# Low parts of w_o and of the second block's routing moved from GpSimd to VectorE

## Chip, cores and metric

One Trainium2 chip, one core. The metric is the device time of one execution in microseconds; lower is better. Times of several executions are given with their median. A profile is one further execution, recorded by the hardware profiler.

## The reference, cut to what matters

A stack of two blocks on 256 tokens of width 1024, in float32. The first is one hybrid layer, the second has two layers, of which the second layer's feed-forward part is a mixture of 8 experts.

```python
# first block
x = x + concat([mla_out, rw_out]) @ w_o                 # w_o: 1024 x 1024
x = x + hier_moe(rms_norm(x, g_ffn), ...)               # 32 small experts
# second block, i = 0, 1
mix = concat([y_pool, y_conv]) @ w_out[i]
x = layer_norm(DEEPNORM_ALPHA * x + mix, ...)
f = swiglu(x, ...) if i == 0 else moe_swiglu(x, ...)
x = layer_norm(DEEPNORM_ALPHA * x + f, ...)
x = x + sigmoid(x @ ple_gate_w[i]) * (p[i] @ ple_w[i])

def moe_swiglu(h, w_router, w1, w3, w2):                # 8 experts of width 3584
    logits = t @ w_router
    top_vals, top_idx = top_k(logits, 2)
    gates = sum(one_hot(top_idx, 8) * softmax(top_vals)[..., None], axis=1)
    for e in range(8):
        out = out + gates[:, e:e+1] * swiglu(t, w1[e], w3[e], w2[e])
```

DEEPNORM_ALPHA is the square root of 2 (4 to the power 0.25).

## The kernel before

Tokens lie on the 128 partitions, in NT = 2 tiles; the residual x is one SBUF tile of 128 x 2 x 1024. Matrix products are made from split operands: `K.split` (L92 to L101) makes a high part `whi` with a Copy on ScalarE (L99), rounded to float32r, and a low part `wlo` = raw - whi with a tensor_tensor on VectorE, or on the engine that it is handed (L100). `mm3` (L113 to L115) then adds three products, high by high, high by low and low by high. With `parts=4` a split is made in four instructions of each engine instead of one. Weights come through `K.load` (L85) into a few `raw` buffers on the SP queue unless another queue is named; a buffer is loaded anew once its readers are done. There are six or fewer raw and two to four split buffers in a stage; in the experts of the second block eight and four.

The program is written with tiles, and a planner that goes by estimated durations puts the instructions of each engine in order; within an engine they then run in that order. `K.behind(list)` (L103) orders the instructions of its block behind the given ones, as far as these are on the same engine.

The stages that the change touches:

- **The end of the first mixer**, `mixer1`. The recurrent half's rows y are normalised (L762 to L771, the last a multiplication with the reciprocal root on VectorE), transposed on TensorE (L776), scaled on ScalarE (L778) and combined on VectorE (L780, L781), and split. Then `w_o(nh, h)` loads and splits quarters of w_o, of 512 rows by 512 columns (tile 128 x 2048). The first two, nh = 0, are made `ahead`, with their low parts on GpSimd. The attention half's rows (L587, L592, L594) are transposed (L794) and split (L796, L797). `finish` multiplies (L113 to L115) and adds into x (L812). The load of w_o(1, 1) is issued from GpSimd's queue. After it come the first block's routing (L899 to L988), its gather (L1046) and its 32 experts (L1074, L1105), whose weights are read unsplit.
- **The routing of the second block's experts**, `moe`. Logits come from TensorE (L1534). `xs` is x split into high and low parts, in rows (L1539, and L1540, L1551, L1552 for the low parts). The logits are transposed (L1545), and `top2` (L833 to L837) finds the two largest of each row, giving A; three small products (L1554 to L1557) count the places, `slot` (L1558, L1559) and `cnt` (L1561). `gather(e)` makes one-hot rows `hot` (L1571) and, in `fill`, 32 matmuls (L1581) that pick an expert's rows, with the high part copied out by ScalarE (L1583) and the low part by VectorE (L1584).
- **The first weight tiles of the experts**, `take`. A tile is 128 x 1792. `jobs` is the list of pairs of tiles in the order of use; `ahead(n)` loads and splits a pair one job before its use. The first two pairs are made before the loop: three of the four tiles with low parts on GpSimd, in pieces of 128 x 448, all but the first behind the high part of xs and the hot rows. Then come the weights of the two experts of each token (`top2_weights`, L846 to L855) and the scaling of x by ALPHA on GpSimd (L1805). The first addition of an expert's result to x (L1661) is at the end of expert 0.

In the experts, `up` multiplies (L1606 if at most 64 tokens are routed to the expert, else L1609), L1837 copies the results out, L1638 turns them, L1822 to L1829 make the hidden rows and L1630 multiplies with w2.

Of the kernel before, what the change touches and what calls it, by code (L numbers as in the profile page):

```python
# [9 lines left out]
F32R = mybir.dt.float32r  # L10
I32 = mybir.dt.int32
U32 = mybir.dt.uint32
AF = mybir.ActivationFunctionType
# [3 lines left out]
ADD, SUB, MUL = ALU.add, ALU.subtract, ALU.mult  # L17
MAX, MIN, EQ = ALU.max, ALU.min, ALU.is_equal

P = 128  # L20
# [3 lines left out]
TOK = 256  # L24
# [151 lines left out]
def mixer1(K, a, x, late, beside):  # L176


    nc, tc = K.nc, K.tc
    with ExitStack() as ctx:  # L180
# [63 lines left out]
        g = nc.gpsimd  # L244
# [32 lines left out]
        for lev in range(6):  # L277
            b = 1 << lev
# [37 lines left out]
        for t in range(NT):  # L316
            ps = K.ps()
            for c in range(KC):
                w = halves[c // 4]
# [9 lines left out]
        for t in range(NT):  # L329
            ps = K.ps()  # L330
# [5 lines left out]
        for c in range(4):  # L336
            ps = K.ps()
            nc.tensor.matmul(ps[:, :TOK], a2[64:128, c * P:(c + 1) * P], lora[64:128, 0, :], start=True, stop=True)
            nc.scalar.activation(ag[:, c, :], ps[:, :TOK], AF.Sigmoid, bias=cols["a0"][:, c:c + 1])
        for c in range(0, 4, 2):  # L340
            ps = K.ps()
# [9 lines left out]
        for c in range(4):  # L351
            ps = K.ps()
# [71 lines left out]
        for t in range(NT):  # L424
            for i, (o, n) in enumerate(((0, 256), (256, 128))):
                z = lat[:, t, o:o + n]
                nc.vector.tensor_scalar(z, z, lss[:, i, t:t + 1], None, op0=MUL)
        for m in range(4):
            ps = K.ps()
# [62 lines left out]
        for i, gcol in enumerate((cols["g_cq"][:, 0:1], cols["g_cq"][:, 1:2], cols["g_ckv"][:, 0:1])):  # L492
            ps = K.ps(ps_mla)
# [109 lines left out]
        for t in range(NT):  # L603
            HG.append(K.t(poolB, [P, 8, P]))
            GR.append([K.t(poolB, [P, 8, 64]) for _ in range(2)])
            for par in range(2):
                for j in range(2):
                    ps = K.ps()
# [164 lines left out]
        for m in range(4):  # L773
# [11 lines left out]
        w_o = lambda nh, h, engine=None: K.split(  # L785
            K.load(a["w_o"][0, h * 512:(h + 1) * 512, nh * 512:(nh + 1) * 512], 4, 512, queue=nc.gpsimd if nh and h else None),
            engine=engine)
        ahead = [w_o(0, h, nc.gpsimd) for h in range(2)]
        attend(1, qT1)
        beside(tmp)  # L790
        for m in range(4):
# [338 lines left out]
class Block2:  # L1130
# [378 lines left out]
    def moe(self, cap=P):  # L1509
# [27 lines left out]
        xs = self.pair((P, NT, D))  # L1537
        for t in range(NT):
            rows = [nc.scalar.activation(xs[0][:, t, :], x[:, t, :], AF.Copy).ins]  # L1539
        nc.gpsimd.tensor_tensor(xs[1][:, 0, :], x[:, 0, :], xs[0][:, 0, :], op=SUB)  # L1540
        lT = self.W([P, 512], "sg", bufs=1)[:E, :TOK]
        nc.vector.tensor_copy(lT, ps[:E, :TOK])
        lg = K.ps()
# [3 lines left out]
        nc.vector.tensor_copy(lt, lg[:, :NT * E].rearrange("p (t e) -> p t e", t=2))  # L1547
        A, comb, slot = self.T([P, NT, E], F32R), self.T([P, NT, E]), self.T([P, NT, E])
        tops = [top2(K, self.tmp, lt[:, t, :], iota, A[:, t, :]) for t in range(NT)]
        with K.behind([tops[1][2]]):  # L1550
            nc.vector.tensor_tensor(xs[1][:, 1, :512], x[:, 1, :512], xs[0][:, 1, :512], op=SUB)  # L1551
        nc.gpsimd.tensor_tensor(xs[1][:, 1, 512:], x[:, 1, 512:], xs[0][:, 1, 512:], op=SUB)  # L1552
        ps = K.ps()
        nc.tensor.matmul(ps[:, :2 * E], K.upper_r, A.rearrange("p t e -> p (t e)"), start=True, stop=False)  # L1554
        nc.tensor.matmul(ps[:, E:2 * E], K.ones_r, A[:, 0, :], start=False, stop=True)
# [11 lines left out]
        def gather(e):  # L1567

            h = self.W([P, NT, P], "hot", F32R)
            for t in range(NT):  # L1570
                self.hot = [nc.vector.tensor_scalar(h[:, t, :], slots, slot[:, t, e:e + 1], None, op0=EQ).ins]  # L1571
            g = self.W([P, KC * TOK], f"xg{e % 2}", F32R, 1).rearrange("p (k i s) -> p k i s", i=2, k=KC)

            def fill():
                for k in range(0, KC, 2):
                    ps = K.ps()
                    for i in range(2):
                        for q in range(2):
                            o = (2 * i + q) * P
                            for t in range(NT):  # L1580
                                nc.tensor.matmul(ps[:, o:o + P], xs[i][:, t, (k + q) * P:(k + q + 1) * P], h[:, t, :],  # L1581
                                                 start=(t == 0), stop=(t == NT - 1))
                    nc.scalar.activation(g[:, k:k + 2, 0], ps[:, :TOK].rearrange("p (q s) -> p q s", s=P), AF.Copy)  # L1583
                    nc.vector.tensor_copy(g[:, k:k + 2, 1], ps[:, TOK:].rearrange("p (q s) -> p q s", s=P))  # L1584
                return g, h
            return fill

# [180 lines left out]
        nc.vector.tensor_copy(cnti, cnt)  # L1768


        def take(n, e, s, k, **how):
            w = K.load(down_of(e, s, k) if n == "down" else up_of(n, e, s, k), 1, MS)
            if n == "down":
                return k, [z[:, 0] for z in (K.split(w) if k < 4 else (w,))]
            b = lambda z: z.rearrange("p k (b q) -> p (k b) q", b=4)
            hl = K.split(b(w), **how)
            return k, [z.rearrange("p b q -> p (b q)") for z in hl]

        jobs = []
        for i in range(E * NS + 1):  # L1780
# [8 lines left out]
        def ahead(n):  # L1789

            if n < len(jobs) and n not in taken:
                name, e, s, ks = jobs[n]
                taken[n] = [take(name, e, s, k) for k in ks]

        for n in range(2):
            name, e, s, ks = jobs[n]
            taken[n] = []
            for i, k in enumerate(ks):
                with K.behind(rows + self.hot if n or i else None):
                    taken[n].append(take(name, e, s, k, parts=PARTS, engine=None if (n, i) == (1, 0) else nc.gpsimd))  # L1800
        gs = {0: fill()}
        for t in range(NT):
            with K.behind(K.last):
                top2_weights(K, self.tmp, *tops[t][:2], iota, comb[:, t, :])
                nc.gpsimd.tensor_scalar(x[:, t, :], x[:, t, :], ALPHA, None, op0=MUL)  # L1805
        fewer = self.T([P, E])
        nc.vector.tensor_scalar(fewer, cnt, HALF + 0.5, None, op0=ALU.is_lt)
        most, mosti = self.T([P, 1]), self.T([P, 1], I32)
# [30 lines left out]

        for n, (name, e, s, ks) in enumerate(jobs):  # L1840
            ahead(n + 1)
            i = NS * e + s
            tiles = taken.pop(n)
            q = min(ks)
            if name == "down":
                if s == 0 and q == 0:
                    accs[e] = [K.ps() for _ in range(2)]
                if i == E * NS - 1 and q == 4:
                    for c in range(0, 2 * R, 4):
                        pts = [K.ps() for _ in range(2)]  # L1850
                        arms(e, lambda few: [turn(few, rows, pt, c) for rows, pt in zip(ups[i], pts)])
                        turned(i, c, pts)
                arms(e, lambda few: [down(few, s, hT[i], accs[e], *t) for t in tiles])
                if s == NS - 1 and q == 0:
                    hotT = transposed(e, gs[e][1])
                if s == NS - 1 and q == 2:
                    if e == E - 1:
                        finish_last(e, accs.pop(e), hotT)
                    else:
                        ends = finish(e, accs.pop(e), hotT)  # L1860
                        next(ends)
                continue
            first = name == "exp_w1_2"
            if (e, s, q, first) == (E - 2, 1, 0, True):
                past()
            if q == 0:
                banks = [K.ps() for _ in range(4)]
            g = gs[e][0]
            before = first and i > 0
            if before:  # L1870
                pts = [K.ps() for _ in range(2)]
                turns = lambda few: [turn(few, rows, pt, 2 * q) for rows, pt in zip(ups[i - 1], pts)]
                if s == 0:

                    arms(e - 1, turns)

            def f(few):
                if before and s:
                    turns(few)
                for t in tiles:  # L1880
                    up(few, e, g, banks, *t)
            arms(e, f)
            if before:
                turned(i - 1, 2 * q, pts)
            if q == 6:
                z = evict(banks, "gs" if first else "us")
                ups.setdefault(i, []).append(z)
                if not first and s == NS - 1 and e + 1 < E:
                    gs[e + 1] = gather(e + 1)()
            if first and q in (2, 6):  # L1890
                next(ends, None)
# [75 lines left out]
```

## Time and profile before

| what | value |
|---|---|
| median of 3 runs | 1967.86 us |
| lowest and highest run | 1962.56, 1967.99 us |
| the profiled execution | 1963.39 us |
| its span in the profile | 1961.8 us |
| TensorE matmul busy | 1768.9 us (90%) |
| VectorE busy | 1315.1 us (67%) |
| ScalarE busy | 1092.3 us (56%) |
| GpSimd busy | 169.4 us (9%) |
| DMA | 546.62 MB, mean 279 GB/s |

Busy times are shares of one span over stages with different limits: an engine that is busy for a ninth of the span can be the only one at work in a short stretch. In the views PE is TensorE, PEld its weight loads, DVE is VectorE, ACT ScalarE, POOL GpSimd, and SPq the DMA queue of SyncE. L12 is line 12 of the kernel; for what a helper issues it is the helper's line, so L99 and L100 are the high and low parts of all splits.

### The profile page before, as it was taken

The page shows a single profiled execution, that of the slowest core. Times are in us where ns is not written, and L with a number is a line of the kernel's source. Part 1 is how long each engine was busy: PE and PEld are TensorE (multiplying, and loading weights), DVE is VectorE, ACT ScalarE, POOL GpSimd, SP SyncE. Part 2 cuts the span into 40 slices and gives each one's busy share as a digit, 9 for nine tenths or more (in the row PEclk, how much of TensorE's full clock was granted, in tenths as well). Part 3 has the DMA queues.
Part 4 walks back from the last instruction along what each step waited for, and adds up shares of the span by engine and source line. Part 5 has one row for each costly group of instructions (what it writes and reads, how often), then busy time and mean ns, then how long its engine had stood idle before and what let it go on. Part 6 is the DMA issues. An engine that isn't in the chain of part 4 may idle for free. (4 is left out here: it accounts for less than half of the span.)

```text
span 1961.8 us, 28227 instructions
## 1 busy us (share of the span) xinstructions
PE 1768.9 (90%) x10999; PEld 1421.1 (72%) x10999; DVE 1315.1 (67%) x1619; ACT 1092.3 (56%) x1446; POOL 169.4 (9%) x250
## 2 busy tenths in 40 slices
PE   7988688778899999889899999998999998888997
PEld 6878474333778999788787687787877778767766
DVE  5675641111886445895886586788978679888877
ACT  6444341001474444555675576677868568777773
POOL 3051210000510000052300000000000000000002
PEclk8989689989999999999899999999999999999999
DMA  7000579999844555334699788999999899999993
GB/s 225 30 1 1 183 311 380 422 421 406 297 142 156 192 193 194 134 103 161 244 323 341 266 330 334 366 337 414 408 375 378 308 356 346 402 374 378 416 392 108
DMA packets 131007, 546.62 MB, mean 279 GB/s; under 512 B 13569, under 2 KB 46476, under 8 KB 118541
## 3 DMA queue, kind: packets, MB, share of 16 engines
q1 hardware_dynamic: 126604, 539.21, 72.3%
q10 hardware_dynamic: 3952, 3.84, 0.6%
q8 instruction: 130, 2.13, 0.4%
q0 software_dynamic: 272, 1.05, 0.2%
q14 instruction: 49, 0.39, 0.1%
HBM read 543.01 MB, written 1.05 MB: 277 GB/s over the span
## 5 line engine op out<-in xcount | busy, mean ns | idle before, releaser
L100 DVE TENSOR_TENSOR wlo<-raw,whi 128x1792 fp32r<-128x1792 f32 (+2 forms) x476 | 811.6, 1736 | 212.5 <-ACT whi L99 207.5
L99 ACT ACTIVATE whi<-raw 128x1792 fp32r<-128x1792 f32 (+3 forms) x500 | 692.5, 1425 | 136.5 <-PE ps L1609 49.3
L1606 PE MATMUL ps<-whi,xg 128*128 128x256 f32 (+1 forms) x960 | 279.1, 319 | 14.0 <-ACT sg L1828 13.4
L1606 PE MATMUL ps<-wlo,xg 128*128 128x256 f32 (+1 forms) x960 | 276.5, 317 | 6.9 <-DVE wlo L100 6.5
L1609 PE MATMUL ps<-whi,xg 128*128 128x512 f32 (+1 forms) x768 | 227.6, 376 | 2.4 <-ACT sg L1828 2.4
L1606 PEld LDWEIGHTS ps<-whi,xg 128*128 128x128 f32 x960 | 196.9, 205 | 27.8 <-ACT sg L1828 15.3
L1606 PEld LDWEIGHTS ps<-wlo,xg 128*128 128x128 f32 x960 | 196.4, 205 | 21.9 <-DVE wlo L100 14.7
L1609 PEld LDWEIGHTS ps<-whi,xg 128*128 128x128 f32 x768 | 143.0, 192 | 30.7 <-ACT sg L1828 2.6
L114 PE MATMUL ps<-xTl,whi 128*128 128x256 f32 x576 | 162.6, 283 | 1.4 <-DVE xTl L100 1.4
L115 PE MATMUL ps<-xTh,wlo 128*128 128x256 f32 x544 | 154.1, 284 | 2.7 <-DVE wlo L100 2.6
L113 PE MATMUL ps<-xTh,whi 128*128 128x256 f32 x544 | 152.4, 283 | 0.4 <-ACT xTh L99 0.4
L1609 PE MATMUL ps<-wlo,xg 128*128 128x512 f32 (+1 forms) x384 | 142.5, 371 | 0.0
L1630 PE MATMUL ps<-raw,hd 128*64 128x512 f32 (+3 forms) x512 | 137.6, 542 | 2.1 <-DVE hd L1829 2.1
L100 POOL TENSOR_TENSOR wlo<-raw,whi 128x448 fp32r<-128x448 f32 (+3 forms) x24 | 39.9, 1688 | 1063.8 <-PE ps L1656 968.9
L114 PEld LDWEIGHTS ps<-xTl,whi 128*128 128x128 f32 x576 | 109.0, 189 | 3.5 <-DVE xTl L100 2.3
L1630 PEld LDWEIGHTS ps<-raw,hd 128*64 128x64 f32 (+1 forms) x512 | 62.8, 158 | 64.6 <-issue 54.5
L115 PEld LDWEIGHTS ps<-xTh,wlo 128*128 128x128 f32 x544 | 103.1, 190 | 5.0 <-DVE wlo L100 4.8
L113 PEld LDWEIGHTS ps<-xTh,whi 128*128 128x128 f32 x544 | 102.7, 190 | 1.7 <-ACT xTh L99 0.9
L1105 PE MATMUL ps<-dn,hT 128*32 128x512 f32 x256 | 69.8, 660 | 19.8 <-DMA dn<-in_w_down_dram 19.7
L1609 PEld LDWEIGHTS ps<-wlo,xg 128*128 128x128 f32 x384 | 73.7, 192 | 13.9 <-issue 0.5
L1822 ACT ACTIVATE odd<-ps,t 128x256 f32<-128x256 f32 (+1 forms) x128 | 53.7, 442 | 36.2 <-PE ps L1638 35.8
L1606 PE MATMUL ps<-wlo,hT 128*128 128x256 f32 (+1 forms) x240 | 67.8, 313 | 5.4 <-issue 2.9
(532 smaller groups left out, 2999.9 us busy)
## 6 DMA issues: line engine op xcount, KB each, us to landing
raw<-in_exp_w_dram SPq DMA_DIRECT2D x384, 896.0 KB
raw<-in_dense_w_dram SPq DMA_DIRECT2D x33, 1024.0 KB
gu<-in_w_up_dram SPq DMA_DIRECT2D x32, 1024.0 KB
dn<-in_w_down_dram SPq DMA_DIRECT2D x32, 1024.0 KB
gu<-in_w_gate_dram SPq DMA_DIRECT2D x29, 1024.0 KB
raw<-in_w_in_dram SPq DMA_DIRECT2D x19, 1024.0 KB
raw<-in_w_out_dram SPq DMA_DIRECT2D x8, 1024.0 KB
raw<-in_ple_gate_w_dram SPq DMA_DIRECT2D x8, 1024.0 KB
```

The lines of the kernel that those rows point to most:

```text
L99: self.last = [nc.scalar.activation(hi[o], src[o], AF.Copy).ins, (engine or nc.vector).tensor_tensor(lo[o], src[o], hi[o], op=SUB).ins]
L100: (engine or nc.vector).tensor_tensor(lo[o], src[o], hi[o], op=SUB).ins]
L113: mm(out, a[0], b[0], start=first, stop=False)
L114: mm(out, a[0], b[1], start=False, stop=False)
L115: return mm(out, a[1], b[0], start=False, stop=last).ins
L1105: nc.tensor.matmul(ps[32 * e:32 * e + 32, :], hT[:, k, 32 * e:32 * e + 32], wd[e][:, k, hs], start=(k == 0), stop=(k == 1))
L1606: mm(to[:, o:o + m], few_rows, w[q][:, i.start + o:i.start + o + m], start=first and o == 0 and q == 0, stop=last and o + m == n and q == 1)
L1609: mm(to, rows[:, a_], w[b_][:, i], start=first and q == 0, stop=last and q == 2)
L1630: mm(to[o], hd[1][:, R + r, ::2 if few else 1], w[0][:, i], start=False, stop=False)
L1822: nc.scalar.activation(odd, z[:, :, :, 1], AF.Copy, scale=fewer[:, i // NS:i // NS + 1])
```

## The change

Low parts of the first two quarters of w_o are made by VectorE. In the second block's routing both low parts of xs are made by VectorE, each right behind its high part in the program's text, with no order demanded. The first four weight tiles are loaded, and split in whole tiles: high parts on ScalarE behind the high part of xs, low parts on VectorE behind the hot rows. For expert 0, the gather's low part is copied out by ScalarE. `top2_weights` stands behind the last of the four low parts. The scaling of x goes to VectorE, in the jobs 4 and 5 of the loop, each behind the newest split.

```diff
-        ahead = [w_o(0, h, nc.gpsimd) for h in range(2)]
+        ahead = [w_o(0, h) for h in range(2)]
...
         for t in range(NT):
             rows = [nc.scalar.activation(xs[0][:, t, :], x[:, t, :], AF.Copy).ins]
-        nc.gpsimd.tensor_tensor(xs[1][:, 0, :], x[:, 0, :], xs[0][:, 0, :], op=SUB)
+            nc.vector.tensor_tensor(xs[1][:, t, :], x[:, t, :], xs[0][:, t, :], op=SUB)
...
         tops = [top2(K, self.tmp, lt[:, t, :], iota, A[:, t, :]) for t in range(NT)]
-        with K.behind([tops[1][2]]):
-            nc.vector.tensor_tensor(xs[1][:, 1, :512], x[:, 1, :512], xs[0][:, 1, :512], op=SUB)
-        nc.gpsimd.tensor_tensor(xs[1][:, 1, 512:], x[:, 1, 512:], xs[0][:, 1, 512:], op=SUB)
...
-                    nc.vector.tensor_copy(g[:, k:k + 2, 1], ps[:, TOK:].rearrange("p (q s) -> p q s", s=P))
+                    low = (g[:, k:k + 2, 1], ps[:, TOK:].rearrange("p (q s) -> p q s", s=P))
+                    if e:
+                        nc.vector.tensor_copy(*low)
+                    else:
+                        nc.scalar.activation(*low, AF.Copy)
...
-        def take(n, e, s, k, **how):
+        def take(n, e, s, k):
...
-            b = lambda z: z.rearrange("p k (b q) -> p (k b) q", b=4)
-            hl = K.split(b(w), **how)
-            return k, [z.rearrange("p b q -> p (b q)") for z in hl]
+            return k, [z[:, 0] for z in K.split(w)]
...
+        raws = [K.load(up_of(name, e, s, k), 1, MS)[:, 0] for name, e, s, ks in jobs[:2] for k in ks]
+        highs, lows = [K.t(K.spl, [P, 1, MS], F32R, tag="whi")[:, 0] for _ in raws], [K.t(K.spl, [P, 1, MS], F32R, tag="wlo")[:, 0] for _ in raws]
+        with K.behind(rows):
+            for w, z in zip(raws, highs):
+                nc.scalar.activation(z, w, AF.Copy)
+        with K.behind(self.hot):
+            for w, z, lo in zip(raws, highs, lows):
+                K.last = [nc.vector.tensor_tensor(lo, w, z, op=SUB).ins]
         for n in range(2):
-            name, e, s, ks = jobs[n]
-            taken[n] = []
-            for i, k in enumerate(ks):
-                with K.behind(rows + self.hot if n or i else None):
-                    taken[n].append(take(name, e, s, k, parts=PARTS, engine=None if (n, i) == (1, 0) else nc.gpsimd))
+            taken[n] = [(k, [highs[2 * n + i], lows[2 * n + i]]) for i, k in enumerate(jobs[n][3])]
         gs = {0: fill()}
         for t in range(NT):
             with K.behind(K.last):
                 top2_weights(K, self.tmp, *tops[t][:2], iota, comb[:, t, :])
-                nc.gpsimd.tensor_scalar(x[:, t, :], x[:, t, :], ALPHA, None, op0=MUL)
...
         for n, (name, e, s, ks) in enumerate(jobs):
             ahead(n + 1)
+            if n in (4, 5):
+                with K.behind(K.last):
+                    nc.vector.tensor_scalar(x[:, n - 4, :], x[:, n - 4, :], ALPHA, None, op0=MUL)
```

## Rows read from the trace of the kernel before

**Rows 1.** The page's first line.

```profile
span 1961.8 us, 28227 instructions
```

**Rows 2.** Busy us by stretch: PE, PEld, DVE, ACT, POOL; granted clock; DMA.

```profile
230.00:235.00 5.00, 0.99 (x4) 0.59 (x4) 5.00 (x1) 0.00 (x0) 4.97 (x2) 0.50 0.89 322
...
290.00:295.00 5.00, 5.00 (x49) 1.79 (x51) 1.68 (x9) 1.85 (x3) 0.00 (x0) 1.00 0.00 0
...
400.00:450.00 50.00, 39.48 (x200) 14.23 (x193) 6.76 (x17) 4.28 (x8) 0.00 (x0) 0.90 1.01 421
...
930.00:940.00 10.00, 0.92 (x6) 0.82 (x6) 9.56 (x16) 3.75 (x7) 9.04 (x8) 0.73 0.29 93
...
950.00:1000.00 50.00, 50.00 (x248) 42.11 (x247) 39.54 (x25) 38.38 (x34) 3.33 (x2) 0.98 0.86 320
```

**Rows 3.** TensorE's waits (total, times, longest) and its timeline before L1554.

```profile
PE ps L776 <- DVE TX L771: 10.3, 2, 5.6
...
PE ps L1606 <- ACT sg L1828: 13.4, 7, 2.4
...
939.26 0.39 PE L1554 MATMUL ps<-t,t 128*128 128x16 f32 x1 [9.08 <-DVE t L837]
```

**Rows 4.** VectorE's timeline, second routing: start, busy us, instruction, idle before.

```profile
939.13 0.68 DVE L1551 TENSOR_TENSOR xTl<-t,xTh 128x512 fp32r<-128x512 f32 x1
...
954.19 2.02 DVE L100 TENSOR_TENSOR wlo<-raw,whi 128x1792 fp32r<-128x1792 f32 x1 [2.23 <-ACT whi L99]
```

**Rows 5.** VectorE's timeline, end of the first mixer.

```profile
226.24 9.44 DVE L771 TENSOR_TENSOR TX<-TX,rstd 128x512 f32<-128x512 f32 x2 [1.20 <-ACT rstd L155]
236.85 0.43 DVE L780 TENSOR_TENSOR fin<-fin,t 128x256 f32<-128x256 f32 x1 [1.17 <-ACT fin L778]
...
254.12 2.29 DVE L100 TENSOR_TENSOR wlo<-raw,whi 128x2048 fp32r<-128x2048 f32 x1 [9.78 <-ACT whi L99]
```

**Rows 6.** GpSimd's timeline, end of the first mixer.

```profile
224.77 4.50 POOL L100 TENSOR_TENSOR wlo<-raw,whi 128x2048 fp32r<-128x2048 f32 x1 [42.80 <-ACT whi L99]
...
230.62 4.50 POOL L100 TENSOR_TENSOR wlo<-raw,whi 128x2048 fp32r<-128x2048 f32 x1
```

**Rows 7.** VectorE's timeline in the first routing.

```profile
276.43 0.29 DVE L942 CAST gf<-gi 128x8 f32<-128x8 uint32 x2
...
277.53 0.31 DVE L833 MAX8 m<-em 128x8 f32<-128x32 f32 x2
...
278.10 1.87 DVE L835 CAST f<-i 128x8 f32<-128x8 uint32 x2
...
280.22 0.41 DVE L837 SCALAR_TENSOR_TENSOR t<-iotf,f,o 128x32 fp32r<-128x32 f32 x2
```

**Rows 8.** ScalarE's timeline at both places.

```profile
226.22 1.89 ACT L99 ACTIVATE whi<-raw 128x2048 fp32r<-128x2048 f32 x1
...
928.94 2.00 ACT L1539 ACTIVATE xTh<-t 128x1024 fp32r<-128x1024 f32 x2 [0.89 <-PE ps L1534]
...
952.46 1.70 ACT L99 ACTIVATE whi<-raw 128x1792 fp32r<-128x1792 f32 x1 [3.81 <-PE ps L1609]
```

**Rows 9.** TensorE's timeline: first w_o matmul, first of the gather, first of expert 0.

```profile
244.40 0.80 PE L113 MATMUL ps<-whi,t 128*128 128x512 f32 x1 [2.20 <-DVE t L797]
...
941.17 1.09 PE L1581 MATMUL ps<-hot,xTh 128*128 128x128 f32 x4 [0.89 <-ACT whi L99]
...
948.03 0.73 PE L1609 MATMUL ps<-whi,xg 128*128 128x512 f32 x1
```

**Rows 10.** Busy us by stretch of 1 us, columns as in rows 2.

```profile
934.00:935.00 1.00, 0.00 (x0) 0.00 (x0) 1.00 (x2) 0.00 (x0) 1.00 (x2) 0.82 0.94 394
...
951.00:952.00 1.00, 1.00 (x5) 0.76 (x5) 0.96 (x2) 0.00 (x0) 1.00 (x1) 0.65 0.69 288
```

**Rows 11.** The chain that ended last: start, us, what.

```profile
1764.62 0.84 PE ps L1581 x8
```

## Prediction

> **What bounds the kernel now.** I read the page first, for the span, then the busy time by stretch, then what TensorE waited for, and only then the timelines of the engines at the two places that the diff touches. The span is 1961.8 us and the profiled execution took 1963.39, so 1.6 us lie around it [rows 1]. Read by stretch, the kernel is a chain of stages with different limits. In the experts of the second block TensorE is busy all the time (50.00 of 50 us from 950), and in the experts of the first block the DMA engines are full (1.01, 421 GB/s). Two short stretches have neither: in 230 to 235 and in 930 to 940 TensorE works about 1 us, while VectorE and GpSimd are both full [rows 2]. The waits say whom TensorE stood for: 10.3 us for VectorE's L771 and 9.1 us, from 930.2 to 939.3, for its L837 [rows 3]. These are two narrow places in a serial chain, so a microsecond saved there is a microsecond of the end, if what follows moves along.
>
> Why VectorE is slow there is to be seen by laying two timelines side by side. L771 is two instructions on 128x512; the same kind and size takes 0.68 us undisturbed [rows 4], here the two take 9.44 [rows 5]. GpSimd's two low parts of 4.50 us run from 224.77 and from 230.62, to 235.12, and L771 ends at 235.68 [rows 6]. So a GpSimd tensor_tensor holds VectorE's instructions up until it ends. The same shows in the first routing: two CASTs of 128x8 take 0.29 us, and beside GpSimd's L955 1.87 [rows 7].
>
> **First edit, the low parts of w_o.** Removed: two GpSimd instructions, and with them the hold-up, 9.44 less 2 x 0.68 = 8.1 us. Added: the same two low parts on VectorE, 2.29 us each by the row of the same shape, together 4.6 us [rows 5]. Where they come in VectorE's order decides. The first high part is there before the square root is; the second only at 226.22 + 1.89 = 228.1 [rows 8]. VectorE has two holes nearby: 1.20 us before L771 and 1.17 us after it, in which it waits for ScalarE [rows 5]. If each low part falls in one hole, 4.6 less 2.4 = 2.2 us stay on the chain and 5.9 are gained; if one hole alone is used, 3.4 stay and 4.7 are gained. Bounds: nothing hidden gains 3.5; all behind the chain gains 8.1. I take 5.3, between the two likely orders. The first w_o matmul then starts at 239.1 instead of 244.40 [rows 9].
>
> Does it reach the end? After w_o come the first block's experts, a stretch bound by DMA, in which a faster engine usually buys nothing. Here the stream is not running when the chain arrives: DMA moves nothing in 290 to 295 and is full later [rows 2]. It stands because all buffers are full until the first expert matmuls free one. That moves with the chain, so the whole stream starts 5.3 us earlier. GpSimd's queue also issues one w_o load behind its first low part; it waits for the same buffer as before, and VectorE frees it no later than about 230. Cost nothing; its tile is the last of the four that the w_o matmuls read.
>
> **Second edit, the routing of the second block.** Removed from GpSimd: the low part of half of xs and a quarter more, twelve pieces of 128x448, and the scaling of x. With GpSimd idle, the VectorE chain from the logits to A runs undisturbed. In the first routing the same instructions, from MAX8 at 277.53 to the end of L837 at 280.63, take 3.1 us, of which the CASTs beside GpSimd are 1.6 too long; so 1.5 us [rows 7]. The copy of the logits before it is another 0.15, by the CASTs.
>
> Added to VectorE: both low parts of xs, 128x1024 each. No row has that shape; between 0.68 for 512 and 2.02 for 1792 columns lies 1.22 [rows 4], two are 2.4 us. Their high parts are done at 929.9 and 930.9 [rows 8], before the logits have gone through, so I put them ahead of the chain. TensorE's wait of 9.1 us becomes 0.15 + 2.4 + 1.5 = 4.1 us, and 5.0 us are gained. Bounds: with the slow 3.1 us for the chain, 3.4; with the low parts wholly behind it, 7.4, but the gather's fifth matmul reads them, so little of that can come.
>
> The gather then starts at 936.2 and the first expert at 943.0 (before 941.17 and 948.03 [rows 9]), if the first four weight tiles are ready. High parts: ScalarE, after rows, 4 x 1.70 = 6.8 us, 930.9 to 937.7 [rows 8], as the gather's first bank comes out. Low parts: VectorE, behind the hot rows, 4 x 2.02 = 8.1 us, 936.2 to 944.3 [rows 4], the first at 938.2. A tile is 12 matmuls, at 50 us for 248 [rows 2] 2.4 us, so the fourth low part has three tiles of cover, some 6 us. Without it, 1.3 us would be lost. The gather's low copies for expert 0 go to ScalarE, four of about the high copies' size, beside the gather. The four raw buffers are freed at 938.2 to 944.3 instead of from 931 on; the SP queue issues the ninth to twelfth load from there, and they are wanted only after four tiles of matmuls. Cost nothing.
>
> Moved: the scaling of x, two VectorE instructions of 128x1024 in expert 0's stream, each below 1.22 us and, if half that, 0.6. VectorE is busy 39.54 of 50 us there and TensorE 50.00 [rows 2], so they lie beside TensorE's work: nothing, and at most 2.4 us without that cover. Behind each stands only the next low part, which is made four tiles ahead.
>
> **The clock.** TensorE's granted clock falls between 934 and 935, some four microseconds after TensorE's wait began at 930.2, and rises between 951 and 952 [rows 10]. [...] With the low clock the sum is 10.3 us, with the high one 15.5, as worked out under the rivals.
>
> **Sum.** 5.3 + 5.0 = 10.3 us. The profiled execution's 1963.4 becomes 1953.1. It stands 4.5 us below the median of the runs, 1967.86, and the runs spread from 1962.56 to 1967.99; against the median the forecast is 1957.6, and as either level can come, I say 1957.
>
> **Rivals.**
> *The clock stays up.* [...] The first tiles' low-clock stretch, 948.0 to 951.6, would halve. That is 3.4 + 1.8 = 5.2 us more: 1952. For it: the wait is halved. Against it: the fall came four microseconds into a wait in this trace.
>
> *A new wait eats the second gain.* Exp of the expert weights on ScalarE now hangs on VectorE instructions that stand behind the four low parts, after 944.3. If ScalarE has it ahead of the gather's evictions, the evictions stand behind it, and the first expert starts little before the 948.03 of now. Likewise if the copy of the counts stands behind four high parts. Price: up to 5.0 us, so 1962.6 against the median. For it: ScalarE does evictions, Exp and high parts from one queue. [...]
>
> *VectorE was not held by GpSimd.* Then nothing is gained: 1968. Against it stands that the same CASTs take 0.29 and 1.87 us.
>
> *Slower: the stream of the second block's experts gets another order.* In it TensorE waits 2.4 us at a time for ScalarE's sg L1828, seven times, 13.4 us in all [rows 3]. The moved instructions change the planned times at its head. If one more such wait comes with each of eight experts, 8 x 2.4 = 19.2 us are lost and 8.9 remain on the wrong side: 1977. It decides from the fifth on (5 x 2.4 = 12 against 10.3). Against it: expert 0 has TensorE as its limit and full buffers, so the streams are the same after it.
>
> **How the numbers follow.** Forecast as summed 0.60 (own range 1953 to 1961), clock up 0.13 (1948 to 1953), second gain eaten 0.17 (1960 to 1964), nothing 0.04, slower 0.06. From 1948 to 1964 the first three hold 0.9; the ends leave the bounds of the unknown prices (8.1 and 7.4) out. The runs spread by 0.28%, so 0.3% (5.9 us) is about what can be told from no change. Faster than 1962.0 are the first two and a fifth of the third: 0.76. Same: the rest of the third and the fourth, 0.17. Slower: 0.07, the last with a little for the unforeseen.
>
> **What would show it.** GpSimd has no instruction between 225 and 235 nor between 925 and 950. L771 takes 0.7 us each, TensorE's wait before L1554 some 4 us, the first w_o matmul lies near 239, the first expert matmul some 10 us before 948.03, near 937.7, counting both gains. DMA in the first experts still starts from 0.00. The prediction is wrong if VectorE's low parts stand ahead of L771 by more than its hole, if the gather waits for ScalarE, or if the shift at 943 is not the shift at the end.

## The result, and the profile after

The changed kernel takes 1956.95 us (median of 7 runs), the kernel before 1966.16 (median of 7 beside them); the medians differ by 9.2 us. One run of the changed kernel took 5734.74 us and is left out of the ratio, which is 0.9945, 95% interval 0.9927 to 0.9963. The means of the runs in it, 1967.07 and 1956.23, differ by 10.8 us. So about 10.8 us are gained, with 7.3 to 14.4 for the interval, where 10.3 were forecast. The profiled execution took 1957.68 us. The page's first line and the row of busy time answer to [rows 1]; GpSimd now works 138.6 us, 169.4 before:

```profile
span 1956.1 us, 28193 instructions
...
PE 1771.1 (91%) x10999; PEld 1422.2 (73%) x10999; DVE 1306.3 (67%) x1620; ACT 1093.0 (56%) x1438; POOL 138.6 (7%) x232
```

The windows of busy time, columns as in [rows 2]:

```profile
230.00:235.00 5.00, 2.43 (x9) 1.62 (x9) 5.00 (x13) 2.77 (x8) 0.40 (x1) 0.50 0.99 398
290.00:295.00 5.00, 3.79 (x40) 1.65 (x36) 1.32 (x5) 0.77 (x2) 0.00 (x0) 1.00 0.34 92
929.00:930.00 1.00, 0.54 (x3) 0.54 (x3) 0.41 (x4) 1.00 (x1) 0.00 (x0) 0.68 0.00 0
930.00:940.00 10.00, 9.11 (x39) 8.71 (x39) 9.38 (x16) 5.74 (x12) 0.00 (x0) 0.50 0.56 185
```

In the two stretches in which TensorE worked about 1 us it now works 2.43 and 9.11. DMA moves nothing from 284 to 292 and has begun again before 295, since the first experts come earlier. The clock falls at 929 to 930, with the gather behind it at 0.50.

VectorE's timeline at the end of the first mixer, which answers to [rows 5]:

```profile
226.40 2.25 DVE L100 TENSOR_TENSOR wlo<-raw,whi 128x2048 fp32r<-128x2048 f32 x1
228.56 1.29 DVE L771 TENSOR_TENSOR TX<-TX,rstd 128x512 f32<-128x512 f32 x2
229.77 2.28 DVE L100 TENSOR_TENSOR wlo<-raw,whi 128x2048 fp32r<-128x2048 f32 x1
231.97 0.75 DVE L780 TENSOR_TENSOR fin<-fin,t 128x256 f32<-128x256 f32 x2
```

L771 takes 1.29 us for its two instructions, 9.44 before. One low part stands in each hole around it. TensorE's timeline at both places, which answers to [rows 3, 9]:

```profile
229.30 2.15 PE L776 MATMUL ps<-t,TX 128*128 128x128 f32 x8 [3.55 <-DVE TX L771]
...
239.40 0.79 PE L113 MATMUL ps<-whi,t 128*128 128x512 f32 x1 [1.62 <-DVE t L797]
...
927.56 0.29 PE L1545 MATMUL ps<-t,sg 8*128 8x8 f32 x2 [3.38 <-DVE sg L1542]
929.46 0.38 PE L1551 MATMUL ps<-t,t 128*128 128x16 f32 x1 [1.62 <-DVE t L837]
...
931.37 1.09 PE L1578 MATMUL ps<-hot,xTh 128*128 128x128 f32 x4 [0.89 <-DVE hot L1568]
...
938.23 0.73 PE L1610 MATMUL ps<-whi,xg 128*128 128x512 f32 x1
```

The wait of 9.1 us before the counts has become two, 3.4 and 1.6 us, and the first expert matmul lies at 938.23 in place of 948.03.

Executions drift: this one was already 1.4 us later than the one before when the first mixer's last head reached TensorE (225.43 against 223.99, both L794), and single experts of the second block differ by up to 5 us between executions of the same instructions (from VectorE's sixth copy of hotT to its seventh, one expert on, 113.5 us in e3 and 118.8 in e1). So what follows is read from marks a short way apart in one execution. Mark A is from that L794 to the first w_o matmul, mark B from the first logits matmul of the second routing (L1534) to the first expert matmul, mark C from the same L1534 to VectorE's first copy of hotT (the turned one-hot rows), which ends expert 0. "Ratio" is to the kernel before, with its interval; a time without one is a single run. Kernels whose instructions are alike in a mark agree there to 0.03 us in A and B and to 0.5 in C (before and e1, 166.94 and 167.40).

```
kernel                       A us     B us      C us   ratio or time
before                      20.41    22.92    166.94
changed                     13.97    18.34    163.14   0.9945 [0.9927, 0.9963]
e1_wo_alone                 13.98    22.93    167.40   0.9968 [0.9955, 0.9981]
e2_routing_alone            20.38    18.33    163.09   0.9982 [0.9970, 0.9994]
e3_gpsimd_reads             23.41       -     163.27   1962.41 us
e4_gpsimd_writes            14.58       -     163.11   1951.37 us
e5_chain_first                 -    15.37    155.38   0.9908 [0.9892, 0.9925]
e6_chain_first_pe_busy         -    13.06    152.57   0.9898 [0.9882, 0.9915]
e8_gather_low_on_vector        -    18.43    163.61   1957.10 us
e9_weight_lows_not_behind      -    25.41    170.13   1968.66 us
e10_lows_in_count_wait         -    16.52    160.64   0.9943 [0.9922, 0.9964]
e6b_pe_busy_alone              -    18.36    162.84   0.9944 [0.9923, 0.9965]
e7_scaling_on_gpsimd           -    20.05    164.06   1958.61 us
```

The first edit shortens A by 6.44 us, the second shortens B by 4.58 and C by 3.80. Together they are 11.0 us up to the first expert matmul and 10.2 up to the end of expert 0. The timed gain of 10.8 agrees with both: the end moves, within the interval, by what the two places give.

### The profile page after: what moved, and what is told of

It reads as the page before. It is cut to its first block, busy times and chain, and to the rows that moved or that the text cites. A ratio compares the mean times of both kernels' runs of the same rounds, so it can differ in the third digit from the quotient of the medians.

```text
span 1956.1 us, 28193 instructions
## 1 busy us (share of the span) xinstructions
PE 1771.1 (91%) x10999; PEld 1422.2 (73%) x10999; DVE 1306.3 (67%) x1620; ACT 1093.0 (56%) x1438; POOL 138.6 (7%) x232
## 5 line engine op out<-in xcount | busy, mean ns | idle before, releaser
L99 ACT ACTIVATE whi<-raw 128x1792 fp32r<-128x1792 f32 (+2 forms) x484 | 684.8, 1454 | 131.9 <-PE ps L1610 45.8
L100 POOL TENSOR_TENSOR wlo<-raw,whi 128x512 fp32r<-128x512 f32 (+1 forms) x10 | 16.5, 1678 | 1042.8 <-ACT whi L99 1042.8
L1607 PE MATMUL ps<-whi,hT 128*128 128x256 f32 (+1 forms) x240 | 66.8, 310 | 4.7 <-issue 3.0
```

The costliest lines, as they stand in the source:

```text
L99: self.last = [nc.scalar.activation(hi[o], src[o], AF.Copy).ins, (engine or nc.vector).tensor_tensor(lo[o], src[o], hi[o], op=SUB).ins]
L100: (engine or nc.vector).tensor_tensor(lo[o], src[o], hi[o], op=SUB).ins]
L1607: mm(to[:, o:o + m], few_rows, w[q][:, i.start + o:i.start + o + m], start=first and o == 0 and q == 0, stop=last and o + m == n and q == 1)
```

## The experiments

The theory: VectorE is held up while GpSimd reads the on-chip memory, and the two gains are those hold-ups less what the low parts cost on VectorE. The rivals: the first block's experts swallow the shift; the gain lies in VectorE's order or in other instructions; TensorE's clock makes it.

**e1_wo_alone and e2_routing_alone: do the parts add?** One edit each, e1 against the kernel before, e2 against the changed one.

```diff
-        ahead = [w_o(0, h, nc.gpsimd) for h in range(2)]
+        ahead = [w_o(0, h) for h in range(2)]
```

```diff
-        ahead = [w_o(0, h) for h in range(2)]
+        ahead = [w_o(0, h, nc.gpsimd) for h in range(2)]
```

> The kernel before with the first edit alone: the w_o low parts of half 0 on VectorE, the second routing as before. If the two parts simply add and what GpSimd's low parts cost is the hold-up of VectorE, the first w_o matmul comes near 239.4 us, 5 to 6.4 us earlier than before, the second routing comes out as before with everything 5 to 6 us earlier (TensorE's wait for the counts still about 9 us, VectorE's copy of the position tiles still about 0.7 us and waiting behind GpSimd), and the time is about 0.3% below before (ratio 0.9967 to 0.9973). The rival that the expert stream of the first block is fixed by its transfers and swallows the shift gives a ratio of 1.000, with the second routing at its old place near 930 us. The rival that the two parts are worth more together than apart (a clock or transfer phase that only both reach) gives less than 0.2%.

> The changed kernel with w_o's low parts back on GpSimd: the second routing's edit alone. If the parts add, VectorE's first copy after the recurrence takes 9 us again and the first w_o matmul comes near 244.4 to 245.7 us; TensorE's waits in the routing are as in the changed kernel (about 3.4 us for the logits' copy, 1.6 us for the counts, 0.9 us for the position tiles) and the time is 4.6 to 5.0 us below before, a ratio of 0.9975 to 0.998. If the low parts in the first mixer's output were worth nothing on the path, the whole gain stands here and the ratio is that of the changed kernel, 0.9945.

Each run has one shortened mark at the changed kernel's value and the other at its value before, to 0.03 us. By the ratios 6.3 and 3.5 us are gained, 9.8 in sum, within the interval of the whole; e2's 0.9982 lies a little above the 0.9975 to 0.998 that was expected. So the parts add and the first block's experts, whose DMA share is 1.01 in 400 to 450 [rows 2], pass the shift on. In e2 the old lines are back, VectorE's first and GpSimd's below it:

```profile
229.43 9.43 DVE L771 TENSOR_TENSOR TX<-TX,rstd 128x512 f32<-128x512 f32 x2 [1.17 <-ACT rstd L155]
```

```profile
227.96 4.50 POOL L100 TENSOR_TENSOR wlo<-raw,whi 128x2048 fp32r<-128x2048 f32 x1 [46.04 <-ACT whi L99]
...
233.80 4.51 POOL L100 TENSOR_TENSOR wlo<-raw,whi 128x2048 fp32r<-128x2048 f32 x1
```

**e3_gpsimd_reads and e4_gpsimd_writes: is it GpSimd, and which of its work?** VectorE makes the low parts as in the changed kernel, and GpSimd does work that nobody needs, once for each of the two quarters of w_o (`r` is the raw quarter, `z` its high part, `dead` a mask that is no longer used). The main lines, e3's first and then e4's:

```diff
+            for o, n in ((0, 896), (896, 896), (1792, 256)):
+                nc.gpsimd.tensor_tensor(dead[:, :n], r[:, o:o + n], z[:, o:o + n], op=SUB)
```

```diff
+            nc.gpsimd.tensor_copy(dead[:, 0:1], ahead[h][0].bitcast(F32)[:, 0, 0:1])
+            for i in range(5):
+                nc.gpsimd.memset(dead, 0.0)
```

> The changed kernel, with GpSimd given work of the old size in the old place that nobody needs: for each half it subtracts the high part from the raw w_o as the kernel before did (pieces of 896, 896 and 256 elements of a partition), and writes the result over a mask that is no longer used. VectorE makes the real low parts as in the changed kernel. If VectorE was held up by GpSimd's instruction that reads the on-chip memory, VectorE's copies at the end of the recurrence (or the low parts beside them) are held up again for several us while GpSimd works, and the first w_o matmul comes 4 to 8 us later than in the changed kernel, at 243 to 248 us; the time goes back by 4 to 8 us. If the gain came from the shape of the instructions on VectorE's side, or from the order of the work alone, with nothing that GpSimd does to VectorE, the first w_o matmul stays near 239.4 us, VectorE's copies take 1.3 us and the time stays near 1957 us.

> The changed kernel, with GpSimd given useless work in the same place that only writes: for each half a copy of one element for the order, then five fills of 896 elements of a partition of the same unused mask. If VectorE is held up only by GpSimd instructions that read the on-chip memory as well, the first w_o matmul stays near 239.4 us and VectorE's copies of the recurrence's end take about 1.3 us each. If any work of GpSimd on the on-chip memory holds VectorE, its copies are drawn out to several us and the first w_o matmul comes later by as much as GpSimd's fills last beside it, 3 to 8 us.

Both came out on the theory's side. With GpSimd reading, A is 23.41 us, 9.4 more than in the changed kernel, where 4 to 8 were expected: here both engines make the low parts, and each holds up the other: VectorE's first low part takes 4.05 us in place of 2.25, GpSimd's 7.28 in place of 4.50 [rows 6]. The single time is 5.5 us longer. The timelines of e3, VectorE's and GpSimd's:

```profile
228.25 4.05 DVE L100 TENSOR_TENSOR wlo<-raw,whi 128x2048 fp32r<-128x2048 f32 x1
232.22 3.68 DVE L771 TENSOR_TENSOR TX<-TX,rstd 128x512 f32<-128x512 f32 x2
235.83 5.11 DVE L100 TENSOR_TENSOR wlo<-raw,whi 128x2048 fp32r<-128x2048 f32 x1
```

```profile
228.08 7.28 POOL L795 TENSOR_TENSOR t<-raw,whi 128x896 f32<-128x896 f32 x3 [46.14 <-ACT whi L99]
```

With GpSimd writing (but for a copy of one element), beside the very same VectorE instructions, nothing but one is held; e4, VectorE's and GpSimd's:

```profile
226.17 2.25 DVE L100 TENSOR_TENSOR wlo<-raw,whi 128x2048 fp32r<-128x2048 f32 x1
228.34 1.29 DVE L771 TENSOR_TENSOR TX<-TX,rstd 128x512 f32<-128x512 f32 x2
...
235.91 1.09 DVE L594 TENSOR_SCALAR t<-t,rstd 128x512 f32<-128x512 f32 x1
```

```profile
226.21 2.65 POOL L795 MEMSET t<- 128x896 f32 x3
...
232.27 4.45 POOL L795 MEMSET t<- 128x896 f32 x5
```

The one is L594, with a single tile as input, 0.48 us in the changed kernel and 1.09 here; it starts inside the last fill, which ends at 236.72. Those 0.6 us are the whole difference in A. So the same low part takes 4.05 us beside GpSimd's reads and 2.25 beside its fills. Why a fill draws out L594 and not the low part, no run shows.

**e9_weight_lows_not_behind: engine or place?** The four weight low parts stay on VectorE, without the order behind the position tiles.

```diff
-        with K.behind(self.hot):
+        with K.behind(None):
             for w, z, lo in zip(raws, highs, lows):
```

> The changed kernel with the four weight low parts of expert 0 on VectorE as they are, but not put behind the position tiles: by the order that results they stand among the instructions of the top two, ahead of the counts. If the place is what matters, the gather starts up to 8 us later than in the changed kernel (near 939 us, about where it was before the change), and the time returns to within 2 us of before, 1963 to 1966 us. If only the engine matters, and GpSimd's hold of VectorE was the whole cost, the gather stays near 931 us and the time near 1957 us.

The place matters as much as the engine. The four low parts slip in among the instructions of the top two, and B is 25.41 us, worse than with GpSimd; the single time of 1968.66 us also lies above the 1963 to 1966 that was expected. TensorE's timeline of e9 has the old wait again, with no GpSimd at work:

```profile
939.93 0.38 PE L1551 MATMUL ps<-t,t 128*128 128x16 f32 x1 [8.61 <-DVE t L837]
```

**e8_gather_low_on_vector: the move priced at nothing.**

```diff
-                    if e:
+                    if True:
                         nc.vector.tensor_copy(*low)
```

> The changed kernel with expert 0's gathered tokens' low parts copied by VectorE, as for all other experts and as before the change, in place of ScalarE. VectorE's four weight low parts stand ahead of them until about 939 us, so the low copies start 3 to 4 us after ScalarE's would have, and the first expert matmul comes at 941 to 944 us in place of 938.2: the move to ScalarE was worth 3 to 5 us on the path, the price that the prediction put at nothing as a move. If the low copies are not what the first matmul waits for, or are put ahead of the weight low parts, it stays within 1 us of 938.2.

The 3 to 5 us of this expectation were wrong, the prediction's nothing was nearly right. VectorE copies the low parts only at 940.75, but the first two expert matmuls read high parts of the tokens, and the third waits 0.23 us; B grows by 0.09. C grows by 0.47, no more than before and e1 differ in it. TensorE's timeline of e8:

```profile
939.83 0.73 PE L1610 MATMUL ps<-whi,xg 128*128 128x512 f32 x1
940.36 0.63 PE L1610 MATMUL ps<-wlo,xg 128*128 128x512 f32 x1
941.22 1.22 PE L1610 MATMUL ps<-whi,xg 128*128 128x512 f32 x2 [0.23 <-DVE xg L1583]
```

**e7_scaling_on_gpsimd: the other move priced at nothing.**

```diff
-            if n in (4, 5):
-                with K.behind(K.last):
-                    nc.vector.tensor_scalar(x[:, n - 4, :], x[:, n - 4, :], ALPHA, None, op0=MUL)
+                nc.gpsimd.tensor_scalar(x[:, t, :], x[:, t, :], ALPHA, None, op0=MUL)
```

(the added line stands beside the top two's weights, as before the change)

> The changed kernel with the residual's scaling of x back where it was, on GpSimd beside the top two's weights, in place of VectorE among the first expert's pieces. If the move cost or gave nothing on the path, the first expert matmul comes 18.3 us after the logits' first matmul as in the changed kernel, and expert 0 ends 163.1 us after it, both within 0.5 us. If GpSimd's reading of x holds VectorE up there as it did in the first mixer, the first expert's first low parts come later and the first expert takes 1 to 5 us more.

Neither line of the expectation gives the place. GpSimd now scales x at 925.74, as soon as its low parts are made, since nothing stands ahead on that engine any more, and that is beside the top two. B grows by 1.7 us. GpSimd's timeline, then VectorE's and TensorE's, of e7:

```profile
925.74 6.42 POOL L1809 TENSOR_SCALAR t<-t 128x1024 f32<-128x1024 f32 x2 [22.38 <-DVE xTl L1540]
```

```profile
927.79 0.24 DVE L833 MAX8 m<-lt 128x8 f32<-128x8 f32 x2
...
928.28 1.17 DVE L835 CAST f<-i 128x8 f32<-128x8 uint32 x2
928.48 1.98 DVE L836 TENSOR_SCALAR o<-iotf,f 128x8 f32<-128x8 f32 x2
```

```profile
930.78 0.38 PE L1551 MATMUL ps<-t,t 128*128 128x16 f32 x1 [3.24 <-DVE t L837]
```

Instructions on 8 columns are held (CAST 1.17 against 0.29 us), MAX8 beside the same GpSimd instruction is not (0.24 us in both kernels). Against this place of GpSimd's scaling, moving it to VectorE's idle time kept 1.6 us of the second gain (the wait before the counts, 3.24 against 1.62); by C, 0.9.

**e5_chain_first and e10_lows_in_count_wait: what the changed kernel leaves.** Of TensorE's 3.4 us before the logits' transposes, VectorE's two x low parts are 2.36. Both runs take them out of the first loop and put them back later; e5 one in the wait for the counts, one behind the position tiles, e10 both in the wait for the counts. The line taken out, then e5's lines, then e10's:

```diff
-            nc.vector.tensor_tensor(xs[1][:, t, :], x[:, t, :], xs[0][:, t, :], op=SUB)
```

```diff
+        with K.behind([tops[1][2]]):
+            nc.vector.tensor_tensor(xs[1][:, 0, :], x[:, 0, :], xs[0][:, 0, :], op=SUB)
...
+        with K.behind(self.hot):
+            self.hot = [nc.vector.tensor_tensor(xs[1][:, 1, :], x[:, 1, :], xs[0][:, 1, :], op=SUB).ins]
```

```diff
+        with K.behind([tops[1][2]]):
+            for t in range(NT):
+                nc.vector.tensor_tensor(xs[1][:, t, :], x[:, t, :], xs[0][:, t, :], op=SUB)
```

> The changed kernel with VectorE's two x low parts of the second routing taken out of the way of the chain: the first stands behind the tokens' top two, while TensorE counts, and the second behind the position tiles, ahead of the weights' low parts. If what is left of TensorE's wait for the logits' copy (3.4 us) is VectorE's 2.36 us of x low parts ahead of it, that wait falls to about 1.0 us, the gather begins about 2.4 us earlier than in the changed kernel, the first expert matmul too (near 935.9 us in a like execution), and the time is 2.4 us lower: a ratio of 0.9933. If the copy waits for something else (the logits' last matmul, ScalarE's copies of x), nothing moves: 0.9945. If the expert stream takes the shift up as a wait for its transfers, the first expert comes earlier but the time stays: 0.9945.

> The changed kernel with both of VectorE's x low parts behind the tokens' top two, in the wait for TensorE's counts, and nothing else moved. The order of all matmuls on TensorE is that of the changed kernel, which it was not in the run with the chain first. If that run's 7 us beyond the changed kernel were 3 us of the chain and 4 to 5 us of the other order of matmuls at the end of the first expert, this one keeps TensorE's wait of 2.7 us there, its first expert matmul comes 1.5 to 2 us earlier after the logits than in the changed kernel, and the ratio to before is 0.9935 to 0.994. If the chain itself was worth the 7 us, most of them come here too: 0.991 to 0.992.

The wait for the logits' copy falls to 0.5 us in both, and B shrinks by 2.97 us in e5, by 1.82 in e10 (whose second low part lies beyond the counts). But C shrinks by 7.8 us in e5, past its expectation. Of the other 4.8, 4.6 lie at the end of expert 0. From the second routing on, the matmuls of before, changed, e1, e2, e4, e8, e9 and e10 stand in the same order on TensorE; in e5 the program's planner of the order has moved 24 weight matmuls there from ahead of a group of hidden-tile transposes to behind it. TensorE's timeline there, of the changed kernel and of e5:

```profile
1058.62 0.65 PE L1639 MATMUL ps<-t,gs 128*128 128x128 f32 x4
...
1069.40 0.66 PE L1639 MATMUL ps<-t,gs 128*128 128x128 f32 x4
...
1073.25 0.70 PE L1639 MATMUL ps<-t,gs 128*128 128x128 f32 x2 [2.70 <-ACT sg L1831]
1075.51 0.67 PE L1639 MATMUL ps<-t,us 128*128 128x128 f32 x2 [1.56 <-DVE hd L1832]
```

```profile
1055.68 0.65 PE L1640 MATMUL ps<-t,gs 128*128 128x128 f32 x4
...
1061.56 0.65 PE L1640 MATMUL ps<-t,gs 128*128 128x128 f32 x4
...
1067.44 0.41 PE L1640 MATMUL ps<-t,gs 128*128 128x128 f32 x2
1069.26 0.48 PE L1640 MATMUL ps<-t,us 128*128 128x128 f32 x2 [1.41 <-DVE hd L1835]
```

The groups lie 10.8 and 3.9 us apart in the one, 5.9 and 5.9 in the other, so the wait of 2.70 us is gone, and with it a fall of the clock (0.74 granted on the mean against 1.00). The windows of both:

```profile
1068.00:1078.00 10.00, 5.74 (x26) 4.38 (x25) 6.74 (x9) 7.13 (x12) 0.00 (x0) 0.74 0.73 252
```

```profile
1066.00:1076.00 10.00, 8.58 (x43) 6.73 (x42) 8.79 (x13) 8.94 (x13) 0.00 (x0) 1.00 0.89 334
```

e10, whose order is the old one, keeps the wait of 2.70 us, gains 2.5 us in C, 0.7 beyond its B, and takes 0.9943. TensorE's timeline of e10:

```profile
1072.90 0.51 PE L1641 MATMUL ps<-t,gs 128*128 128x128 f32 x2 [2.70 <-ACT sg L1833]
```

So the chain was worth some 2 to 3 us beyond the changed kernel, and e5's 0.9908 is for the larger part luck of the planner. That e10's timed gain over the changed kernel is no larger than its interval leaves the 2 us to the marks alone.

**e6_chain_first_pe_busy and e6b_pe_busy_alone: the clock.** Matmuls that nobody reads are put into TensorE's waits: four in e6, with e5's order, and five in e6b, with the changed kernel's. The line that issues them:

```diff
+                    dead = nc.tensor.matmul(idle, K.ident, x[:, 0, :512], start=True, stop=True).ins
```

> The kernel of the run with the chain first, with four matmuls of 128 by 512 that nobody reads added on TensorE, where it waits in the second routing: one after the logits, two after their transposes, one after the counts. If TensorE's clock falls there because it has little to do, it stays at its upper level, the gather's 32 matmuls take about 3.5 us in place of 6.9 and the first up tiles 1.8 in place of 3.6: up to 5.2 us less than without them, a ratio near 0.9907. If the clock falls all the same, or the added matmuls stand in the way of the chain, the ratio is that of the run without them (0.993) or worse by up to their own 2 to 4 us (0.995).

> The changed kernel with five matmuls of 128 by 512 that nobody reads on TensorE in its waits of the second routing: three after the logits, one after their transposes, one after the counts; VectorE's order is as in the changed kernel, and so is TensorE's apart from them. If the clock stays at its upper level through the gather, the gather's matmuls take 4.2 us in place of 6.9 as they did in the run before with such matmuls, and the first expert's first matmul comes 2.3 to 2.7 us earlier after the logits; the prediction priced this rival at 5.2 us, which would be a ratio of 0.9919, and the run before it suggests 2.5 to 3 us, 0.993. If the clock falls all the same, the ratio stays at 0.9945 or a little above.

In e6 no wait of TensorE between the logits and the first expert matmul is longer than 0.29 us, and the clock stays up (1.00). In e6b waits of 0.76 and 0.57 us are left, and it falls at 935 to 936 (0.92 there, 0.50 behind). The windows of e6, then of e6b:

```profile
925.00:935.00 10.00, 9.46 (x73) 6.73 (x70) 6.54 (x22) 8.49 (x8) 0.00 (x0) 1.00 0.09 37
```

```profile
935.00:936.00 1.00, 0.90 (x5) 0.74 (x6) 0.26 (x3) 1.00 (x1) 0.00 (x0) 0.92 0.00 0
936.00:937.00 1.00, 1.00 (x3) 0.29 (x1) 0.96 (x5) 1.00 (x3) 0.00 (x0) 0.50 0.00 0
```

So the clock at 1.00 is worth 2.3 us in B and 2.8 in C (e6 against e5), about half of the 5.2 that the prediction gave this rival: the gather still takes 4.2 us, where the author's estimate was 3.4, and of the 1.8 us for the first tiles 0.5 shows. By the timed ratios, 0.9898 and 0.9908, it cannot be told from nothing. e6b gains nothing.

## Why the prediction was right, point by point

**First edit.** Right in its mechanism, small in its size. Forecast 5.3 us, measured 6.44 by A. The hold-up of 8.1 less 6.4 gives 1.7 us of the low parts' 4.53 that stay on the chain, where the sum left 2.2 to 3.4. The middle between two orders was taken, and the better one, 5.9, came: both holes were used. The low part ahead of L771 takes 2.25 us in a hole of 1.20, which the prediction names as a sign of being wrong; but its own better order has it so, and L771 starts only 0.88 us later for it (3.13 us after L794 in place of 2.25), where the sum had 1.1. The other half a microsecond is made of such tenths, as from L780 to the first w_o matmul, 7.43 us in place of 7.55. The first w_o matmul, forecast at 239.1, lay at 239.40, with 1.4 us of drift in between.

**The first block passes the shift on.** Right: L1534 starts 5.2 us earlier in the profiled execution (919.89 against 925.11), and e1's whole ratio is the first edit's 6.3 us. From the first w_o matmul to L1534 it is 680.7 us before, 680.5 after and 682.3 in e1, so single executions show it to within 2 us.

**Second edit.** Right to 0.4 us at the first expert matmul: forecast 5.0, measured 4.58. The wait for the counts was forecast at 0.15 + 2.4 + 1.5 = 4.1 us. Measured are 3.38 + 1.62, less the 0.5 that TensorE waits for the logits' copy in any case, 4.5. The low parts do stand ahead of the chain, and they take 2.36 us. That little could come of putting them later was wrong: the gather's fifth matmul reads them, but e5 has one made in the wait for the counts and one under the first gather matmuls, and gains 3 us.

What the prediction did not see is that only 3.80 of the 4.58 us reach the end of expert 0 (C; e2 has 3.85). The clock rises again between 943 and 944, 4.8 us into expert 0, where before it rose between 951 and 952 [rows 10], 3 to 4 us in; at the transposes of 1058.62 (1067.93 before) 4.09 us are left. The changed kernel's windows at the rise:

```profile
942.00:943.00 1.00, 1.00 (x5) 0.90 (x5) 0.32 (x2) 0.00 (x0) 0.00 (x0) 0.50 0.97 358
943.00:944.00 1.00, 1.00 (x6) 0.83 (x5) 0.00 (x0) 0.89 (x1) 0.00 (x0) 0.99 0.98 410
```

**The sum.** By the marks the first edit gave 1.1 us more than forecast and the second 0.4 to 1.2 less, so that the two misses nearly cancel in the 10.3. That the median lies 0.05 us from the 1957 of the forecast is luck: 1957 was counted from a median of 1967.86, and with seven runs that median is 1966.16.

**What was priced at nothing.** The gather's low copies: 0.1 us at the first expert matmul by e8, and by C no more than the spread. The scaling: on VectorE it costs nothing that shows, on GpSimd it would have cost 1.7 us at the first expert, in the place that e7 gave it.

**The clock and the rivals.** The clock fell all the same, 929 to 930 (0.68 granted in that microsecond, 0.50 behind it), so the sum with the low clock held. The rival with the clock up did not occur, and its price of 5.2 us was twice what e6 shows. No run shows its term of 3.4 us for the gather: with the clock at 1.00 the gather took 4.2 us in e6, against 6.9 in the kernel before (941.17 to 948.03 [rows 9]). The second gain was not eaten: ScalarE copies the counts at 930.73, does all evictions by 939.1, and loads the table for Exp only then. ScalarE's timeline of the changed kernel:

```profile
930.73 0.18 ACT L1558 ACTIVATE t<-ps 128x8 f32<-128x8 f32 x1 [0.24 <-DVE t L1555]
...
938.75 0.38 ACT L1585 ACTIVATE xg<-ps 128x256 fp32r<-128x256 f32 x1
939.15 1.28 ACT L847 ACT_TABLE_LOAD   x1
```

VectorE was held by GpSimd: L771 took 9.43 us in e2 and 3.68 in e3, 1.29 in the changed kernel. The slower rival did not occur here, since the orders of matmuls in the second block and of SP's loads are unchanged, but its mechanism is real: e5's order differs by such a move and is worth some 4.6 us, with the sign the other way.

**What stays open.** The prediction calls itself wrong if the shift at 943 is not the shift at the end. In the one profiled pair it is not: 9.8 us at the first expert matmul, 9.0 after expert 0 and 5.7 at the end; in e4 the last two are 9.4 and 12.0. The later experts' lengths wander by up to 5 us between executions with the same order, and no run isolates why. So a single pair cannot decide this sign; the timed gain of 7.3 to 14.4 us speaks for the shift, and is no sharper than that.

The hold-up is also longer than GpSimd's record. In the kernel before, the second L771 is recorded from 229.74, 0.9 us ahead of GpSimd's second low part at 230.62 [rows 6], and takes 5.94 us; in e2 the two start at 232.94 and 233.80. No run shows what holds VectorE before GpSimd's start. VectorE's timeline of before:

```profile
229.74 5.94 DVE L771 TENSOR_TENSOR TX<-TX,rstd 128x512 f32<-128x512 f32 x1
```

## What to carry to other kernels

Where VectorE stands on the serial chain, look for GpSimd instructions that read the on-chip memory beside it: in this kernel two instructions of 4.5 us there cost two short ones of VectorE 8.1 us, and making the same numbers on VectorE in a wait that it has anyway is cheaper, though twice 2.3 us. Moving work is half of it; where it lands in the order is the other half, and at the first expert matmul the second edit gains 4.6 us with its four weight low parts behind the position tiles and loses 2.5 with them among the top two. When an edit gains more than its place can give, compare the order of instructions far behind it before crediting the edit.

## What the runs showed of the hardware

Beside GpSimd's fills of 226.21 to 228.86 (e4) VectorE's low part took 2.25 us, and L771, which starts under them at 228.34, 1.29, both as in the changed kernel; beside its subtractions into the same tile (e3) they took 4.05 and 3.68. Cutting GpSimd's instruction into three did not free VectorE (e3): GpSimd's 2048 columns took 7.28 us in place of 4.50 and VectorE's 4.05 in place of 2.25. Five extra matmuls in TensorE's waits did not save its clock where waits of 0.76 and 0.57 us were left between them (e6b: 0.50 granted in 936 to 937); four did where the longest was 0.29 (e6: 1.00 from 925 to 935).
